# Way down of a SwiGLU network by seven products over all 22 tiles of h, with sums on GpSimd and raw stores

## The chip, the cores and the metric

The kernel runs on one core of one Trainium2 chip. The metric is device time in microseconds (us), the median of several runs; lower is better. The time before is 1420.02 us (three runs, 1419.3 to 1420.16).

A core has five engines, each with its own queue that it works off strictly in order: TensorE (PE in the profile: matrix products, with PEld for its weight loads), VectorE (DVE), ScalarE (ACT), GpSimd (POOL) and SyncE (SP), which here issues every DMA. Engines wait for each other by semaphores. TensorE writes its products into PSUM, which has eight banks of 128x512 floats; everything else on chip lies in SBUF, in tiles of 128 partitions by 1024 floats.

## The reference, cut to what matters

One layer of an encoder: two attention branches, a gated merge, an output projection, a LayerNorm, and then a SwiGLU network with a second LayerNorm. The change lies in the last three lines:

```python
x = layer_norm(DEEPNORM_ALPHA * x + mix, ln1_g[l], ln1_b[l])       # (1024, 1024)
gu = x @ w_ffn_in[l]                                               # the way up: (1024, 5632)
g, u = jnp.split(gu, 2, axis=-1)
ffn = (jax.nn.silu(g) * u) @ w_ffn_out[l]                          # the way down: h (1024, 2816) @ (2816, 1024)
x = layer_norm(DEEPNORM_ALPHA * x + ffn, ln2_g[l], ln2_b[l])
```

## The kernel before, in words

**Products.** Every product of floats is made of three products of rounded parts: an operand a is split into a high part (a cast on ACT) and a low part (a minus its high part, a subtraction), and hi*hi, hi*lo and lo*hi are added up in PSUM. `split` (L109 to L111) is that pair: `scalar.copy` on ACT, `tensor_tensor` subtract on DVE. Two blocks by two blocks are multiplied by seven block products in place of eight (the variant of Strassen's scheme by Winograd): the operands are first added and subtracted in a chain of four sums a side, and the seven products, numbered 1 to 7 here, are then added into the results. Part of the adding is left to PSUM: products 1, 6, 7 and 4 run on in one bank ("sx", "dx"), 5 and 3 in another ("sz", "dz"), and each intermediate value is read out of the bank between two of them.

**Way up** (`up_steps`, `pair_steps`, `run_pairs`). The 22 tiles of h (128 rows of h transposed, 1024 tokens wide; f = 0 to 21) are made one after the other. f = 0 is made by plain products, each other f by seven products of 12 matmuls each, in the order 1, 2, 6, 5, 7, 3, 4 (`pair_steps`, L183 to L231). Product 5 writes the bank "sz"; ACT copies it out (`p5`, COPY gt<-szf, L212); product 3 goes on in the same bank, so it waits for that copy. While f is multiplied, the weights of the next tiles are loaded by SP and made ready: the right-hand block wRf comes in by one DMA (L142), and its quarter wcf is cast on ACT (`prep_last`, CAST wcf<-wRf). After product 4 of f the last half of h is finished on ACT and DVE (L1306, L1307).

**Between the two.** h does not fit beside the rest, so it goes to DRAM. For the 16 tiles f = 2 to 17 (eight pairs, four groups of two in `SEVEN`) `left_sums` makes the left-hand sums of the pair (f, f + 1) with four subtractions or additions on DVE, splits each of the seven sums on ACT and DVE, and stores high and low parts side by side. The work of a pair is cut into 11 `pieces`; `next_piece` runs one of them after each product of the way up. f = 0, 1 and 18 to 21 are stored as they are (`h_dr`).

**Way down** (L1438 on). Tiles 0 and 1 are multiplied plainly (`down_plain`, eight tiles of 128 tokens, both halves of 512 columns), then the four groups of `SEVEN` by `down_seven`: a group is two pairs, taken twice (two token tiles of each half at a time), 7 products of 2 x 12 matmuls. The stored left sums are loaded ready for use (`load_left`), the right sums are made on chip a group ahead (`right_sums`, one sum of a pair on GpSimd, L1485, the others on DVE). DVE adds every bank into the sum of x and the result (`add_to`, L1460). Tiles 18 to 21 come last, plainly; with each of the eight token tiles done, its LayerNorm follows (`layer_norm`): statistics and one scaling on DVE, one scaling on ACT and one addition on GpSimd (L1195); the last tile ends on DVE alone.

**What sets the order.** The program is recorded line by line and a scheduler then orders the instructions of each engine by what it expects to be ready; a slot in SBUF or a bank in PSUM that is used again makes its new writer wait for the last reader. A GpSimd operation that overwrites a tile also waits until a DMA that stores that tile has read it.

Of the kernel before, what the change touches and what calls it, by code (L numbers as in the profile page):

```python
# [18 lines left out]
P = 128  # L19
# [29 lines left out]
def hybrid_trunk_kernel(ctx: ExitStack, tc, x, xt, w_first, w_v, w_in, b_gate, rel_bias, w_proj,  # L49
# [51 lines left out]
    h_dr = dram("h_dr", NF)  # L101


    SEVEN = [(f0, f0 + 2) for f0 in (2, 6, 10, 14)]
    ORDER = (1, 2, 6, 5, 7, 3, 4)
    s_dr = [[dram(f"s_dr{g}_{hf}_", 7) for hf in range(2)] for g in range(4)]
# [1070 lines left out]
    def layer_norm(t, g, b, name, quick, done=lambda cs: None, n_st=2, cuts=(LO, HI)):  # L1177
# [3 lines left out]
        for j in range(n_st):  # L1181
            nc.vector.bn_stats(st[:, 6 * j:6 * j + 6], t[:, j * w:(j + 1) * w])
            if j == 0:
                nc.vector.tensor_scalar(st[:, 2:3], st[:, 2:3], EPS * D, None, ALU.add)
# [96 lines left out]
    def plain_rest():  # L1281
        plain_half(HI, ops_21 + ops_1[4])
        dma(h_dr[0], first_h[1])

    def up_steps(f):
# [13 lines left out]
        def done(name, acc):  # L1299
            if name == "11":  # L1300
                nc.scalar.activation(c("11"), c("11"), AF.Silu)
            elif name == "12":
                nc.vector.tensor_tensor(c("12"), c("12"), c("11"), ALU.mult)
            elif name == "21":
                h = tl["h"]
                nc.scalar.activation(h[:, HI], acc, AF.Silu)  # L1306
                nc.vector.tensor_tensor(h[:, HI], h[:, HI], c("22"), ALU.mult)  # L1307
                if f in pair_of:
                    h_tiles[f] = h
                    if f % 2:  # L1310
                        pieces.extend(left_sums(f - 1))
                else:
                    dma(h_dr[f], h)
# [4 lines left out]
    pair_of = {f + d: (g, i) for g, fs in enumerate(SEVEN) for i, f in enumerate(fs)  # L1318
               for d in range(2)}
    h_tiles, pieces = {}, []  # L1320

    def left_sums(f):

        g, i = pair_of[f]
        a, b = h_tiles.pop(f), h_tiles.pop(f + 1)

        def out(p, src):
            def piece():
                o = slot("op", f"sl{f}_{p}", F32R)
                o4 = o.rearrange("p (t k c) -> p t k c", t=2, k=2)  # L1330
                split(o4[:, :, 0, :], o4[:, :, 1, :], src.rearrange("p (t c) -> p t c", t=2))
                for hf, cs in enumerate((LO, HI)):
                    dma(s_dr[g][hf][ORDER.index(p)][:, i * HW:(i + 1) * HW],
                        o[:, cs].bitcast(F32))
            return piece

        def put(dst, in0, in1, op):
            return lambda: nc.vector.tensor_tensor(dst, in0, in1, op)
# [7 lines left out]
    def next_piece(i):  # L1346
        if pieces:
            pieces.pop(0)()
# [91 lines left out]
    acc_t = [slot("op", f"x1_{tt}") for tt in range(8)]  # L1440

    def load_plain(f0, f1, tags):
        hs = []
        take = lambda name, dtype: cycle(tags, name, dtype)
        for f in range(f0, f1):
            hs.append(load_w(h_dr[f], f"h{f}", of("gt"), take, nc.vector) +
                      load_w(w_ffn_out[f * P:(f + 1) * P, :], f"fo{f}", of("gt"), take,
                             nc.vector))
        return hs

    def down_plain(hs, tt, evac, cuts=((0, HW), (HW, D))):
        ts_ = slice(tt * P, (tt + 1) * P)
        for n, (c0, c1) in enumerate(cuts):
            cs = slice(c0, c1)
            acc = bank(("mm", "tr", "sc")[n], f"fps{hs[0][0].name}_{tt}_{n}")[:, 0:c1 - c0]
            mm3(acc, [(hh[:, ts_], hl[:, ts_], oh[:, cs], ol[:, cs]) for hh, hl, oh, ol in hs])
            evac(acc_t[tt][:, cs], acc)

    def add_to(dst, acc):
        nc.vector.tensor_tensor(dst, acc, dst, ALU.add)  # L1460

    def right_sums(g, Ws, tags):

        def take(name):
            return cycle(tags, name, F32R)

        def split_to(W, key, src, nm):
            W[key] = take(f"{nm}h"), take(f"{nm}l")
            split(*W[key], src)

        def load(f, tag, cs):
            t = slot(tag, f"wd{tag}{f}")
            for j, dst in enumerate((LO, HI)):
                dma(t[:, dst], w_ffn_out[(f + j) * P:(f + j + 1) * P, cs])
            return t

        sub = ALU.subtract
        put = nc.vector.tensor_tensor
        for f, W in zip(SEVEN[g], Ws):

            L, R = load(f, "gt", LO), load(f, "yt", HI)
            split_to(W, "12", L, f"wdl{f}")
            yield
            put(L[:, LO], R[:, LO], L[:, LO], sub)
            nc.gpsimd.tensor_tensor(R[:, LO], R[:, HI], R[:, LO], sub)  # L1485
            yield
            c = W["c"] = take(f"wdc{f}")
            split(c[:, LO], c[:, HI], R[:, HI])
            yield
            put(R[:, HI], R[:, HI], L[:, LO], sub)  # L1490
            put(L[:, HI], L[:, HI], R[:, HI], sub)
            yield
            split_to(W, "54", L, f"wda{f}")
            yield
            split_to(W, "76", R, f"wdb{f}")
            yield

    def load_left(g, hf):
        ls = {}
        for n, p in enumerate(ORDER):  # L1500
            t = ls[p] = cycle(LEFT, f"sd{g}_{hf}_{p}", F32R)
            dma(t.bitcast(F32), s_dr[g][hf][n])
        return ls

    def down_seven(g, hf, Ws, ls, between):

        bx, by = {}, {}
        key = {1: ("12", LO), 2: ("12", HI), 5: ("54", LO), 4: ("54", HI), 7: ("76", LO),
               6: ("76", HI)}
        for p in ORDER:  # L1510
            for j in range(2):
                tt = 2 * hf + j
                nm = f"{g}_{tt}"
                up, lo = acc_t[tt], acc_t[tt + 4]
                if p == 1:
                    bx[j] = bank(("mm", "tr")[hf], f"dx{nm}")
                elif p in (2, 5):
                    by[j] = bank("sc" if p == 5 else ("tr", "pv")[j], f"d{'yz'[p == 5]}{nm}")
                acc = by[j] if p in (2, 5, 3) else bx[j]
                first = p in (1, 2, 5)  # L1520
                for i, W in enumerate(Ws):
                    if p == 3:
                        wh, wl = W["c"][:, LO], W["c"][:, HI]
                    else:
                        wh, wl = (w[:, key[p][1]] for w in W[key[p][0]])
                    o = i * HW + j * P
                    lh, ll = ls[p][:, o:o + P], ls[p][:, o + 256:o + 256 + P]
                    for n, (a, b) in enumerate(((lh, wh), (lh, wl), (ll, wh))):
                        mm(acc, a, b, start=(first and i == n == 0), stop=(i == n - 1 == 1),  # L1529
                           skip_group_check=not first)  # L1530
                for dst in {1: [up[:, LO]], 2: [up[:, LO]], 6: [up[:, HI]], 5: [lo[:, HI]],
                            7: [lo[:, HI]], 3: [up[:, HI]], 4: [lo[:, LO]]}[p]:
                    add_to(dst, acc)
            between()

    LEFT = ("bw",) * 4 + ("kp",) + ("bw",) * 5 + ("kp",) * 3
    right_tags = [QKV * 2 + ("pt",) * 4 + ("xt",) * 2, ("xt",) * 14]
    first = load_plain(0, 2, ("bw", "bw", "kp", "kp", "bw", "bw", "bw", "kp"))
    Wd = [[dict(), dict()] for _ in SEVEN]
    make = right_sums(0, Wd[0], right_tags[0])  # L1540
    for tt in range(8):
        dma(acc_t[tt], x1_dr[tt])
        down_plain(first, tt, lambda dst, acc: nc.vector.scalar_tensor_tensor(
            dst, dst, ALPHA, acc, ALU.mult, ALU.add))
        for _ in range(2):
            with tc.issue_after(added[0].ins):
                next(make, None)
    left = load_left(0, 0)
    for g in range(4):
        if g < 3:  # L1550
            make = right_sums(g + 1, Wd[g + 1], right_tags[(g + 1) % 2])
        for hf in range(2):
            ls = left
            if (g, hf) != (3, 1):
                left = load_left(g + hf, 1 - hf)
            down_seven(g, hf, Wd[g], ls, lambda: next(make, None))
    last = load_plain(18, NF, QKV * 2 + ("pt",) * 4 + ("bw",) * 4)
    norm2 = [bcast(src, slot("yt", f"ln2{n}")) for src, n in ((ln2_g, "g"), (ln2_b, "b"))]
    for tt in range(8):
        end = tt == 7  # L1560
# [46 lines left out]
```

## Time and profile before

| what | value |
|---|---|
| median of three runs | 1420.02 us (1419.3 to 1420.16) |
| span of the profiled execution | 1418.4 us |
| PE busy | 1408.0 us, 99% of the span |
| DVE busy | 1054.1 us, 74% |
| ACT busy | 684.7 us, 48% |
| POOL busy | 246.5 us, 17% |
| DMA | 276.54 MB, mean 195 GB/s |

The span runs from the first to the last instruction of the profiled execution; the page gives no other time of it. PE is busy in all but 10.4 us of the span, some 7 of them after its last matmul. The other engines' busy time costs nothing as long as PE never waits for it.

### The profile page before, as it was taken

What the parts mean: (1) busy time and instruction counts of PE and PEld (TensorE: products, weight loads), DVE (VectorE), ACT (ScalarE), POOL (GpSimd) and SP (SyncE); (2) the same over time, 40 slices, a digit from 0 to 9 for tenths busy, and PEclk for the clock granted to TensorE, in tenths of its full rate; (3) what the DMA queues carried; (4) which work ended last, traced back from release to release, by engine and by line L of the source; (5) the groups of instructions that cost most, each with busy time, mean ns of one, the idle gap of its engine ahead of it and who ended that gap; (6) DMA issues with size and microseconds to landing.
All of it is one profiled execution on the core that took longest, in us unless ns stands there. A gap on an engine that the chain in (4) does not pass through costs nothing.

```text
span 1418.4 us, 19023 instructions
## 1 busy us (share of the span) xinstructions
PE 1408.0 (99%) x6672; PEld 1171.7 (83%) x6672; DVE 1054.1 (74%) x1669; ACT 684.7 (48%) x1193; POOL 246.5 (17%) x318
## 2 busy tenths in 40 slices
PE   9999999999999999999999999999999999999997
PEld 7888888888888888888888888888888888888886
DVE  8967657535887778878998947777676656978757
ACT  6544444555888887874424624444344433212201
POOL 0000000002656888840001000000000000100014
PEclk9999999999999999999999999999999999999999
DMA  7486468846676469656651214444334458787502
GB/s 253 163 291 223 169 250 306 293 180 220 220 234 191 148 235 304 242 178 219 228 191 60 89 60 163 157 148 156 135 147 164 159 182 288 278 314 238 202 15 104
DMA packets 104974, 276.54 MB, mean 195 GB/s; under 512 B 10400, under 2 KB 26784, under 8 KB 104880
## 3 DMA queue, kind: packets, MB, share of 16 engines
q1 hardware_dynamic: 104880, 275.35, 55.4%
q8 instruction: 52, 0.85, 0.2%
q14 instruction: 42, 0.34, 0.1%
HBM read 179.33 MB, written 92.30 MB: 192 GB/s over the span
## 4 chain that ended last, share of the span: by engine, by line
PE 91%; DVE 2%; DMA 2%; ACT 1%; issue 1%; POOL 1%; SPq 0%; DVEq 0%; POOLq 0%; ACTq 0%
PE sxf L180 16%; PE sxp L180 9%; PE szf L180 8%; PE dx L1529 6%; PE v L482 5%; PE szp L180 4%; PE syf L180 4%; PE gps L607 4%; PE dz L1529 3%; PE ops L1375 3%; PE yAps L911 3%; PE syp L180 2%; PE tp_a L818 2%; PE tp_b L818 2%; PE fpswh_h L118 2%; PE fpswh_h L117 2%
## 5 line engine op out<-in xcount | busy, mean ns | idle before, releaser
L1485 POOL TENSOR_TENSOR wdyt<-wdyt 128x512 f32<-128x512 f32 x8 | 11.2, 1404 | 512.8 <-DMA sd<-s_dr 443.6
L795 POOL TENSOR_TENSOR w_b<-w_b,kp_b 128x511 f32<-128x511 f32 (+3 forms) x96 | 96.1, 1014 | 23.5 <-DVE kp_b L790 17.0
L790 DVE TENSOR_TENSOR_SCAN kp_b<-kp_b,ident_ps 128x512 f32<-128x512 f32 (+2 forms) x64 | 56.5, 885 | 21.2 <-ACT kp_b L787 20.3
L787 ACT ACTIVATE kp_b<-sc_b 128x512 f32<-128x512 f32 (+3 forms) x96 | 48.1, 501 | 28.0 <-PE sc_b L707 20.9
L180 PE MATMUL szf<-x1S63h,wcf 128*128 128x512 f32 x168 | 55.1, 389 | 0.0
L111 DVE TENSOR_TENSOR pt_b<-tp_b,pt_b 128x512 fp32r<-128x512 f32 (+1 forms) x96 | 49.9, 544 | 6.6 <-ACT pt_b L110 5.7
L730 POOL MEMSET bias<- 64x64 f32 x2 | 0.3, 144 | 313.7 <-ACT bias L726 313.7
L1460 DVE TENSOR_TENSOR x<-dx,x 128x512 f32<-128x512 f32 x64 | 43.4, 686 | 14.9 <-PE dx L1529 14.9
L111 DVE TENSOR_TENSOR sl<-h,sl 128x512 fp32r<-128x512 f32 x56 | 38.4, 686 | 20.5 <-ACT sl L110 20.5
L110 ACT CAST sl<-h 128x512 fp32r<-128x512 f32 x56 | 34.7, 619 | 36.9 <-PE syf L180 17.1
L760 POOL TENSOR_SCALAR w_a<-w_a,st_a 128x640 f32<-128x640 f32 (+2 forms) x64 | 42.2, 667 | 50.4 <-PE sc_a L707 27.0
L110 ACT CAST pt_b<-tp_b 128x512 fp32r<-128x512 f32 (+1 forms) x96 | 46.6, 502 | 8.2 <-PE tp_b L818 8.0
L1186 POOL TENSOR_TENSOR mv<-mv,neghalf 128x1 f32<-128x1 f32 x16 | 12.2, 760 | 220.6 <-DVE mv L1185 220.5
L1306 ACT ACTIVATE h<-sxf 128x512 f32<-128x512 f32 x21 | 12.6, 598 | 77.0 <-PE sxf L180 77.0
L755 ACT ACTIVATE w_a<-w_a,st_a 128x640 f32<-128x640 f32 (+2 forms) x64 | 44.7, 699 | 8.6 <-DVE st_a L749 7.5
L788 ACT ACTIVATE w_b<-sc_b 128x511 f32<-128x511 f32 (+3 forms) x96 | 48.2, 502 | 0.0
L818 PE MATMUL tp_b<-ident,w_b 128*128 128x128 f32 x288 | 47.3, 272 | 0.4 <-DVE pt_b L111 0.2
L111 DVE TENSOR_TENSOR pt_a<-tp_a,pt_a 128x512 fp32r<-128x512 f32 (+1 forms) x96 | 44.6, 485 | 3.3 <-ACT pt_a L110 2.2
L818 PEld LDWEIGHTS tp_b<-ident,w_b 128*128 128x128 f32 x288 | 36.4, 140 | 11.3 <-DVE pt_b L111 1.3
L110 ACT CAST pt_a<-tp_a 128x512 fp32r<-128x512 f32 (+1 forms) x96 | 39.3, 430 | 11.5 <-PE tp_a L818 10.6
L818 PE MATMUL tp_a<-ident,w_a 128*128 128x128 f32 x240 | 42.9, 275 | 0.4 <-DVE pt_a L111 0.3
L607 PE MATMUL gps<-xl,wh_g 128*128 128x512 f32 x96 | 41.7, 434 | 0.0
(1789 smaller groups left out, 4815.2 us busy)
## 6 DMA issues: line engine op xcount, KB each, us to landing
s_dr<-sl SPq DMA_DIRECT2D x112, 256.0 KB, 2.3
sd<-s_dr SPq DMA_DIRECT2D x56, 512.0 KB, 4.9
wLf<-in_w_ffn_in_dram SPq DMA_DIRECT2D x22, 512.0 KB, 4.3
wRf<-in_w_ffn_in_dram SPq DMA_DIRECT2D x22, 512.0 KB, 3.6
v_dr<-vc SPq DMA_DIRECT2D x16, 512.0 KB, 3.2
qs<-q_dr SPq DMA_DIRECT2D x16, 512.0 KB, 6.6
kh<-k_dr SPq DMA_DIRECT2D x16, 512.0 KB, 5.7
kl<-k_dr SPq DMA_DIRECT2D x16, 512.0 KB, 7.1
```

The lines of the kernel that those rows point to most:

```text
L110: return (nc.scalar.copy(dst_h, src), nc.vector.tensor_tensor(dst_l, src, dst_h.bitcast(F32), ALU.subtract))
L111: nc.vector.tensor_tensor(dst_l, src, dst_h.bitcast(F32), ALU.subtract))
L180: mm(acc, lw[:, ks], rx, start=(first and kt == i == 0), stop=(kt == 3 and i == 2), skip_group_check=not first)
L482: mm(accs[j], a, b, start=(first and kt == n == 0), stop=(kt == 3 and n == 2), skip_group_check=True)
L607: mm(acc[hf], lw[:, ks], rx[k][:, (LO, HI)[hf]], start=(k == j == 0), stop=(k == KT - 1 and j == 2))
L755: nc.scalar.activation(s[:, 0:w], s[:, 0:w], AF.Exp, bias=st[:, m:m + 1], scale=-1.0, accum_out=st[:, 2:3])
L787: nc.scalar.activation(kp[:, c0:e], sc[:, 0:n], AF.Sigmoid, scale=-1.0)
L788: nc.scalar.activation(be[:, m0:e], sc[:, m0 - c0:n], AF.Sigmoid)
L790: nc.vector.tensor_tensor_scan(kp[:, 0:e], kp[:, 0:e], ident_ps()[:, 0:e], 0.0, ALU.mult, ALU.add)
L795: nc.gpsimd.tensor_tensor(be[:, m0:e], be[:, m0:e], kp[:, m0 - 1:e - 1], ALU.mult)
L818: ins = tr(tp[:, (qb - lo_q) * P:(qb - lo_q + 1) * P], wt[qb - q0][:, (kb - qb) * P:(kb - qb + 1) * P], ident)
L1529: mm(acc, a, b, start=(first and i == n == 0), stop=(i == n - 1 == 1), skip_group_check=not first)
```

## The change

- All 22 tiles of h now go through seven products: 11 pairs in `GROUPS` of 3, 4 and 4 pairs. A group runs its seven products in the order 1, 2, 5, 3, 6, 7, 4, each over all pairs of the group and four tiles of tokens (`steps`, 21 of them). `down_plain`, `down_seven`, `load_plain` and `h_dr` are gone.
- The left sums of all 11 pairs are made on GpSimd, and they are stored raw, not split: a half as large store for each of the seven. `next_piece` runs two pieces at a time.
- On the way down each raw sum is loaded two steps ahead (`load_left`), cast on ACT and its low part subtracted on GpSimd (`left_piece`). The right sums are made and split one step ahead (`right_piece`).
- All four banks of a kind are held through a group. Group 0's first read of each sum scales x by alpha (`take_down`).
- The LayerNorms of token tiles 0 to 3 follow product 6 of the last group, those of tiles 4 to 7 product 4, the last product; the last one is taken in two halves of 256 columns in the same bank.
- `w_ffn_out` is laid out on the host so that one load brings a pair's two blocks.

```diff
+    GROUPS = ((0, 3), (3, 7), (7, 11))
+    ORDER = (1, 2, 5, 3, 6, 7, 4)
...
         def out(p, src):
-            def piece():
-                o = slot("op", f"sl{f}_{p}", F32R)
-                o4 = o.rearrange("p (t k c) -> p t k c", t=2, k=2)
-                split(o4[:, :, 0, :], o4[:, :, 1, :], src.rearrange("p (t c) -> p t c", t=2))
-                for hf, cs in enumerate((LO, HI)):
-                    dma(s_dr[g][hf][ORDER.index(p)][:, i * HW:(i + 1) * HW],
-                        o[:, cs].bitcast(F32))
-            return piece
+            return lambda: dma(s_dr[g][p][:, i * HW:(i + 1) * HW], src)
         def put(dst, in0, in1, op):
-            return lambda: nc.vector.tensor_tensor(dst, in0, in1, op)
+            return lambda: nc.gpsimd.tensor_tensor(dst, in0, in1, op)
         a_lo, a_hi, b_lo, b_hi = a[:, LO], a[:, HI], b[:, LO], b[:, HI]
         return [out(1, a_lo), out(4, b_hi),
                 put(b_hi, a_hi, b_hi, ALU.add), put(a_hi, a_lo, a_hi, ALU.subtract),
...
     def next_piece(i):
-        if pieces:
-            pieces.pop(0)()
+        for _ in range(2):
+            if pieces:
+                pieces.pop(0)()
...
+    def left_piece(s, i):
+        g, p = steps[s]
+        src = left_raw[s][i]
+        o = slot("xt", f"sl{g}_{p}_{i}", F32R)
+        nc.scalar.copy(o[:, LO], src)
+        nc.gpsimd.tensor_tensor(o[:, HI], src, o[:, LO].bitcast(F32), ALU.subtract)
+        lefts.setdefault(s, []).append(o)
+
+    def right_piece(s, i):
+        g, p = steps[s]
+        sub, put = ALU.subtract, nc.vector.tensor_tensor
+        L, R = raw[g, 0][i], raw[g, 1][i] if p not in (1, 2) else None
+        if p == 5:
             put(L[:, LO], R[:, LO], L[:, LO], sub)
+        elif p == 3:
             nc.gpsimd.tensor_tensor(R[:, LO], R[:, HI], R[:, LO], sub)
+        elif p == 6:
             put(R[:, HI], R[:, HI], L[:, LO], sub)
+        elif p == 4:
             put(L[:, HI], L[:, HI], R[:, HI], sub)
+        t, cs = {1: (L, LO), 2: (L, HI), 5: (L, LO), 3: (R, HI), 6: (R, HI), 7: (R, LO),
+                 4: (L, HI)}[p]
+        o = cycle(RIGHT, f"wd{g}_{p}_{i}", F32R)
+        split(o[:, LO], o[:, HI], t[:, cs])
...
+    for s, (g, p) in enumerate(steps):
+        n = GROUPS[g][1] - GROUPS[g][0]
...
+        if s + 2 < len(steps):
+            load_left(s + 2)
...
+        todo = prepare(s + 1) if s + 1 < len(steps) else []
...
+        for j in range(4):
...
+            for cs in (slice(0, 256), slice(256, HW)) if end else (LO,):
+                for i in range(n):
+                    lh, ll = (lefts[s][i][:, c:c + HW][:, ts_] for c in (0, HW))
+                    wh, wl = (rights[s][i][:, c:c + HW][:, cs] for c in (0, HW))
+                    for k, (a, b) in enumerate(((lh, wh), (lh, wl), (ll, wh))):
+                        mm(accs[j][:, cs], a, b, start=(first and i == k == 0),
+                           stop=(i == n - 1 and k == 2), skip_group_check=not first)
+                take_down(g, p, j, accs[j], cs)
+            for _ in range(-(-len(todo) // (4 - j))):
+                todo.pop(0)()
+            if s < 3:
+                next_piece(0)
+            if last and p in (6, 4):
+                tt = j + 4 * (p == 4)
+                layer_norm(acc_t[tt], *norm2, f"2_{tt}", end,
...
```

What the scheduler makes of this, at three places.

SP's queue on the way up, from the load of wRf15 on. In these names wRf and wLf are weight blocks, s_dr a stored left sum, sl12_5 a split sum before (pair 12 and 13, product 5), h12 and h13 the tiles that the sums are made in now. Before:

```order
L142 DMA wRf15_10072<-in_w_ffn_in_dram 128x1024
L131 DMA wLf16_10111<-in_w_ffn_in_dram 128x1024
L1333 DMA s_dr2_0_2_187<-sl10_6_9973 128x512
L1333 DMA s_dr2_1_2_194<-sl10_6_9973 128x512
L1333 DMA s_dr2_0_5_190<-sl10_3_9992 128x512
L1333 DMA s_dr2_1_5_197<-sl10_3_9992 128x512
L1333 DMA s_dr2_0_0_185<-sl12_1_10052 128x512
L1333 DMA s_dr2_1_0_192<-sl12_1_10052 128x512
L1333 DMA s_dr2_0_6_191<-sl12_4_10091 128x512
L1333 DMA s_dr2_1_6_198<-sl12_4_10091 128x512
L142 DMA wRf16_10219<-in_w_ffn_in_dram 128x1024
```

and now:

```order
L141 DMA wRf15_9881<-in_w_ffn_in_dram 128x1024
L130 DMA wLf16_9917<-in_w_ffn_in_dram 128x1024
L1325 DMA s_dr1_2_143<-h13_9807 128x512
L1325 DMA s_dr1_4_148<-h13_9807 128x512
L1325 DMA s_dr1_5_144<-h13_9807 128x512
L1325 DMA s_dr1_7_147<-h12_9678 128x512
L1325 DMA s_dr1_6_146<-h12_9678 128x512
L1325 DMA s_dr1_3_145<-h13_9807 128x512
L141 DMA wRf16_10014<-in_w_ffn_in_dram 128x1024
```

The load of wRf16 stood behind the first two sums of the pair (12, 13); it now stands behind all of that pair's sums, the last of which needs all four of GpSimd's operations.

ACT's queue at the same place, in f = 14 (gt14<-szf14 is the copy of product 5 that product 3 waits for, wcf16 the cast of a quarter of wRf16). Before:

```order
L208 COPY h14_10130<-sxf14_10057 128x512
L110 CAST sl12_2_10180<-h13_9990 128x2x256
L212 COPY gt14_10070<-szf14_10133 128x512
L110 CAST sl12_7_10199<-h12_9843 128x2x256
L110 CAST wcf16_10235<-wRf16_10219 128x512
```

and now:

```order
L109 CAST waf15h_9893<-taf15_9883 128x1024
L207 COPY h14_9937<-sxf14_9866 128x512
L109 CAST wcf16_10030<-wRf16_10014 128x512
L211 COPY gt14_9879<-szf14_9941 128x512
L109 CAST wlf17h_10050<-wLf17_10048 128x1024
```

The cast of wcf16 has moved ahead of the copy of gt14. The same pair of rows stands so in f = 4, 6, 8, 10, 12, 14, 16 and 18, eight times; in the odd ones the copy comes first.

DVE's queue in the first group of the way down (x1_2 is token tile 2 of the sum, d2_0_2 the bank of product 2 in group 0 for that tile, wd0_6_0 the low part of the right operand of product 6, pair 0). Before, in the first group of `down_seven`:

```order
L1460 TENSOR_TENSOR x1_0_11134<-dy0_0_11406,x1_0_11134 128x512
L1460 TENSOR_TENSOR x1_1_11135<-dy0_1_11414,x1_1_11135 128x512
L111 TENSOR_TENSOR wda6l_11474<-wdgt6_11396,wda6h_11473 128x1024
L1460 TENSOR_TENSOR x1_0_11134<-dx0_0_11380,x1_0_11134 128x512
L111 TENSOR_TENSOR wdb6l_11492<-wdyt6_11399,wdb6h_11491 128x1024
```

and now:

```order
L1499 TENSOR_TENSOR x1_1_10872<-d2_0_1_11022,x1_1_10872 128x512
L110 TENSOR_TENSOR wd0_6_0_11161<-wd1_0_10897,wd0_6_0_11161 128x512
L110 TENSOR_TENSOR wd0_6_1_11178<-wd1_1_10898,wd0_6_1_11178 128x512
L110 TENSOR_TENSOR wd0_6_2_11195<-wd1_2_10899,wd0_6_2_11195 128x512
L1499 TENSOR_TENSOR x1_2_10873<-d2_0_2_11040,x1_2_10873 128x512
L110 TENSOR_TENSOR wd0_7_0_11225<-wd1_0_10897,wd0_7_0_11225 128x512
L1499 TENSOR_TENSOR x1_3_10874<-d2_0_3_11055,x1_3_10874 128x512
L110 TENSOR_TENSOR wd0_7_1_11241<-wd1_1_10898,wd0_7_1_11241 128x512
L110 TENSOR_TENSOR wd0_7_2_11257<-wd1_2_10899,wd0_7_2_11257 128x512
L110 TENSOR_TENSOR wd1_1_3_11408<-wd0_6_11145,wd1_1_3_11408 128x512
L1496 SCALAR_TENSOR_TENSOR x1_4_10875<-x1_4_10875,d5_0_0_11073 128x512
```

Seven subtractions from SBUF now stand ahead of the first read of product 5 (d5_0_0), whose bank product 3 goes on in.

More of the change, by code (lines that the diff above doesn't have):

```diff
@@ L1459, in add_to @@
[L1459 to L1483, printed above, removed]
+    raw_tags = ((("gt",) * 3, ("kp",) * 3), (("yt",) * 3 + ("bw",), ("gt",) * 3 + ("pt",)),
+                (("kp",) * 4, ("yt",) * 3 + ("bw",)))
@@ L1495, in right_sums @@
[L1495 to L1534, printed above, removed]
```

149 lines of the change are left out of this document (79 added, 70 removed).

## The prediction

> **What bounds the kernel now.** I read the page first, then the busy time by stretches, then the chain that ended last, then single instructions around the places that the change touches.
>
> ```profile
> span 1418.4 us, 19023 instructions
> ...
> PE 1408.0 (99%) x6672; PEld 1171.7 (83%) x6672; DVE 1054.1 (74%) x1669; ACT 684.7 (48%) x1193; POOL 246.5 (17%) x318
> ...
> POOL 0000000002656888840001000000000000100014
> ```
>
> PE is busy in all but 10.4 us of the span. GpSimd does nothing from slice 24 to 33: that is the whole way up, where the change now gives it work. The stretches (way up, the two plain tiles, the seven-product groups, the last tiles):
>
> ```profile
> core 0: us, PE busy (x) PEld busy (x) DVE busy (x) ACT busy (x) POOL busy (x), PEclk, DMA share, GB/s
> 821.50:1160.00 338.50, 338.50 (x1495) 279.99 (x1494) 231.32 (x317) 140.22 (x212) 0.00 (x0) 1.00 0.41 148
> ...
> 1214.00:1367.00 153.00, 153.00 (x677) 126.58 (x676) 119.38 (x164) 28.51 (x30) 8.41 (x6) 1.00 0.66 234
> 1367.00:1418.00 51.00, 44.04 (x206) 36.80 (x204) 37.23 (x62) 8.07 (x7) 21.18 (x15) 0.98 0.21 83
> ```
>
> PE has no gap on the way up nor in the groups, at the full clock (1.00). So a product less is a gain, and any new wait of PE is a loss, each at its full length. The chain that ended last, around f = 16:
>
> ```profile
> 1038.16 5.44 PE sxf L180 x24
> 1043.60 2.72 PE syf L180 x12
> ...
> 1054.48 2.72 PE szf L180 x12
> ```
>
> Twelve matmuls take 2.72 us, 0.2267 each. The first row is product 4 of f = 15 and product 1 of f = 16, which starts at 1040.88; product 3 of f = 16 starts at 1054.48, 13.60 us later.
>
> **Products saved.** Before, the way down has 96 matmuls for tiles 0 and 1, 672 in the groups and 192 for tiles 18 to 21, counted as 512 columns each: 960. Now 7 products x 11 pairs x 4 token tiles x 3 are 924. The 36 saved are 36 x 0.2267 = **-8.2 us**. DVE also loses the splits of the left sums on the way up, worth nothing, since PE does not wait there.
>
> **The shared way into SBUF.** The new work is on GpSimd, beside DVE. What the two do to each other stands in the timeline of before:
>
> ```profile
> 1217.38 1.62 POOL L1485 TENSOR_TENSOR wdyt<-wdyt 128x512 f32<-128x512 f32 x1 [10.68 <-DVE wdgt L1484]
> 1217.77 0.68 DVE L1460 TENSOR_TENSOR x<-dx,x 128x512 f32<-128x512 f32 x1
> ...
> 1258.46 0.68 DVE L111 TENSOR_TENSOR wdc<-wdyt,wdc 128x512 fp32r<-128x512 f32 x1
> 1258.68 1.63 POOL L1485 TENSOR_TENSOR wdyt<-wdyt 128x512 f32<-128x512 f32 x1 [14.65 <-DVE wdgt L1484]
> ...
> 1293.25 0.68 DVE L1460 TENSOR_TENSOR x<-dx,x 128x512 f32<-128x512 f32 x1
> 1293.46 1.29 POOL L1485 TENSOR_TENSOR wdyt<-wdyt 128x512 f32<-128x512 f32 x1 [11.36 <-DVE wdgt L1484]
> 1293.85 1.46 DVE L111 TENSOR_TENSOR wdc<-wdyt,wdc 128x512 fp32r<-128x512 f32 x1
> 1295.23 0.68 DVE L1460 TENSOR_TENSOR x<-dx,x 128x512 f32<-128x512 f32 x1
> 1295.83 0.68 DVE L1490 TENSOR_TENSOR wdyt<-wdyt,wdgt 128x512 f32<-128x512 f32 x1
> ```
>
> A read of a bank (x<-dx,x) keeps its 0.68 us beside GpSimd. A subtraction with both operands in SBUF does not: begun 0.39 us into GpSimd's 1.29, it takes 1.46, the rest of GpSimd's operation and then its own time. The other way round GpSimd, begun 0.22 into DVE's, takes 1.63, its own 1.29 and what was left of DVE's. So each holds the other off for a whole operation: 1.29 us on GpSimd, 0.60 on DVE (the last two rows start 0.60 apart). I call this the port.
>
> [...] The rows show it at 512 columns alone; if 1024-wide subtractions held GpSimd only as long as these, 0.60, the wait of the next paragraph would be 2.4 us in place of 3.4.
>
> **Way up: a wait in every second tile.** The order shows wRf of the next even tile behind all stores of a pair's sums on SP, and its cast ahead of the copy on ACT that product 3 waits for. The links, from the rows of f = 15 and 16:
>
> ```profile
> 1040.92 0.60 ACT L1306 ACTIVATE h<-sxf 128x512 f32<-128x512 f32 x1 [5.41 <-PE sxf L180]
> 1041.55 0.69 DVE L1307 TENSOR_TENSOR h<-h,gt 128x512 f32<-128x512 f32 x1 [1.93 <-ACT h L1306]
> 1049.01 1.22 DVE L111 TENSOR_TENSOR wbf15l<-tbf,wbf15h 128x1024 fp32r<-128x1024 f32 x1
> 1050.75 1.22 DVE L111 TENSOR_TENSOR waf15l<-taf,waf15h 128x1024 fp32r<-128x1024 f32 x1
> 1051.80 0.59 ACT L212 COPY gt<-szf 128x512 f32<-128x512 f32 x1 [0.36 <-PE szf L180]
> 1056.04 0.62 ACT L110 CAST wcf<-wRf 128x512 fp32r<-128x512 f32 x1 [1.74 <-DVE sl L111]
> ```
>
> ```profile
> s_dr<-sl SPq DMA_DIRECT2D x112, 256.0 KB, 2.3
> ...
> wRf<-in_w_ffn_in_dram SPq DMA_DIRECT2D x22, 512.0 KB, 3.6
> ```
>
> Counted from the start of the even tile's product 1 (1040.88): the odd tile's h is done at 1.4 (1041.55 + 0.69). Its upper half is stored; GpSimd's first sum overwrites that half and waits for the store, 2.3 us (to 3.7). Four sums of 1.29 with 0.1 of handing over each are 5.6 (9.3); that hand-over is my estimate (L1306's end and L1307's start are 0.03 apart, product 5's end and the copy L212 0.04, and a semaphore to SP and back is longer). DVE's two 1024-wide subtractions (1.22) fall among them, at 8.1 and 9.9 in these rows, and hold them up by 1.1 each (11.5). The last store is issued, about 0.4, then the load (11.9), which lands 3.6 later (15.5). The cast takes 0.62, the copy 0.59, with some 0.3 of handing over: 17.0. Product 3 was due at 13.6. So PE waits **3.4 us**, eight times (f = 4, 6, ..., 18): **+27 us**. Behind the waiting cast on ACT stands only that copy; behind the stores on SP stand wRf and the next wLf, which has time. In before the same copy ran at 1051.80, ahead of the cast at 1056.04: nothing waited. From below: no wait at the port (-2.2) and the shortest chain otherwise (-0.5) leave 0.7 each, 5.6 in all; from above: a load as slow as 4.6, with two more wide subtractions' ends in the way, 4.5 each, 36.
>
> **Start of the way down: port-bound.** After f = 21's product 1 frees the first slots (2.72 us from that tile's start), load and cast bring GpSimd's first subtraction at about 6. By the order, up to DVE's first read of product 5, which product 3 needs, GpSimd has 23 operations (4 of them the sums of the last pair) and DVE some 26 subtractions with both operands in SBUF: 23 x 1.29 + 26 x 0.60 = 45.3 us of port. So that read ends at 6 + 45.3 + 0.7 = 52. PE would be there at 19.04 (f = 21) + 3 products x 36 x 0.2267 (8.16) = 43.5. **+9 us** (0 if the port's queue is packed around PE's needs, 14 if every hand-over costs 0.1 more).
>
> **Rest of the way down.** For a group of four pairs, port time is GpSimd 28 + 4 operations x 1.29 = 41.3 and DVE 28 + 12 x 0.60 = 24.0, 65.3 us beside 76.2 of PE. So the debt of group 0 is not passed on much; while it is worked off I put **+5** (0 to 15: at the upper end one step in two of the 14 waits for 2 us).
>
> **The tail.** The last tiles of before end so:
>
> ```profile
> 1409.89 2.37 POOL L1195 TENSOR_TENSOR x<-x,ln2b 128x1024 f32<-128x1024 f32 x1 [2.04 <-ACT x L1194]
> ...
> 1410.77 0.28 PE L120 MATMUL fpswh_h<-wh_fo,wl_h 128*128 128x256 f32 x1
> ...
> 1412.07 0.26 DVE L1185 BATCH_NORM_AGGREGATE mv<-bn 128x2 f32<-128x24 f32 x1
> ...
> 1412.41 0.55 POOL L1186 TENSOR_TENSOR mv<-mv,neghalf 128x1 f32<-128x1 f32 x1
> ...
> 1413.78 1.41 DVE L1190 SCALAR_TENSOR_TENSOR x<-x,mv,ln2b 128x512 f32<-128x512 f32 x2
> ```
>
> ```profile
> L1182 DVE BATCH_NORM_STATS2 bn<-x 128x6 f32<-128x512 f32 x14 | 9.7, 695 | 0.5
> L1187 DVE SCALAR_TENSOR_TENSOR x<-x,mv,ln2g 128x1024 f32<-128x1024 f32 x8 | 10.5, 1307 | 0.3
> ```
>
> Before, 7.4 us pass from the last matmul's end (1410.77 + 0.28) to the end of the span, 3.2 of them behind DVE's last scaling, and a token tile has 5.44 us of PE to cover its LayerNorm. Now tiles 4 to 7 get 2.72 each in the last product, while DVE stays behind: by its order, between the end of tile 4's matmuls and the read of tile 7's first half stand 3 reads (0.60), 5 statistics (0.7), 5 small ones (0.26) and 2 scalings (1.31), 9.2 us. So that read begins at 2.72 + 0.3 + 9.2 = 12.2 after the product's start. Tile 7's second half uses the same bank and waits for it (0.4), then takes 12 x 0.113: PE ends at 14.0 in place of 4 x 2.72 = 10.9, +3.1. Then the port: the two last GpSimd additions (2.37) and DVE's scaling of tile 7 between them exclude each other, and GpSimd's power for tile 7 stands behind both: 14.0 + 2.37 + 1.31 + 2.37 + 0.55 = 20.6, then 1.41 on DVE and 3.2 for the last store, 25.2. Before's pattern would give 10.9 + 7.4 = 18.3. **+7** (2 to 9).
>
> **Sum.** -8.2 + 27 + 9 + 5 + 7 = +39.8, on the profiled 1418.4: 1458.2. The median of the runs lies 1.6 above that span, so 1459.8; I give 1460.
>
> **Rivals.** *The port costs little*: GpSimd and DVE run side by side. Then the way up has 5.6, the start of the way down nothing, the tail its wait for the bank: -8.2 + 5.6 + 3.1 = +0.5, 1420.5. For it speaks that the reads of banks are not slowed; against it stand the rows with 1.46 and 1.63.
>
> *Faster*: as that, and wRf lands in time. The place is product 3 of the even tiles, the price 8 x 0.7, and it decides at 13.6 us: a chain of 14.3 without the port needs only 0.7 less, such as sums that follow each other without hand-over (0.4) and a store of 2.0. Then -8.2 + 3.1 gives 1415. It needs the port to be free, so it is unlikely.
>
> *Half*: the subtractions of DVE fall beside the sums and not among them. The way up costs 8 x 1.2, group 0 half, the rest 2: -8.2 + 9.6 + 4.5 + 2 + 6 = +14, 1434.
>
> *Port-bound to the end*: over the whole way down the port has 92 x 1.29 + 110 x 0.60 = 185 us, and the last LayerNorms add 7 x (2.37 + 1.2) = 25: 210 beside 924 x 0.2267 = 209 of PE. If hand-overs cost 0.1 in each of these 200, the way down is 20 longer: 1480.
>
> **How the numbers follow.** Forecast (1445 to 1472) 0.63, half 0.15, to the end 0.13, little port 0.05, faster 0.04. The range takes the forecast's bounds and the nearer part of both neighbours: 1437 to 1475. Below about 0.2% (2.8 us) a difference from no change can't be told here. Faster 0.04, within 0.2% 0.03 (most of the little-port case), slower 0.93.
>
> **What would show it.** Right: in the profile after, PE has gaps of about 3.4 us before product 3 of f = 4, 6, ..., 18, ended by ACT's copy, whose engine waited for wRf's DMA; DVE subtractions of 512 columns on the way down take up to 1.9; PE waits at product 3 of group 0 for DVE; the last matmul lies some 10 us before the end. Wrong: no gap on the way up (the load came in time), or DVE subtractions of 0.68 beside GpSimd's operations, or a way down whose length is 209 us and no more.

## The result, and the profile after

The changed kernel takes 1470.01 us (median of four runs, 1465.44 to 1471.84) beside 1420.09 us for the kernel before: a ratio of 1.0345, 95% interval 1.0326 to 1.0364. It is 50 us slower; the profiled execution has a span of 1470.1 us, 51.7 more than before.

From the page of the changed kernel, the busy times and GpSimd's busy tenths:

```profile
PE 1424.1 (97%) x6636; PEld 1179.0 (80%) x6636; DVE 1023.9 (70%) x1563; ACT 698.6 (48%) x1247; POOL 450.5 (31%) x442
...
POOL 0000000004557797700010111110011114866656
```

PE has 36 matmuls less and is busy 16 us longer. That is the first odd thing; a wait alone does not make PE busier. To see where, I cut both kernels at the same matmuls: way up from f = 1, way down, and what follows the last matmul. The columns are those of the prediction's stretches; behind the five engines' busy times stand the granted clock, the DMA share and GB/s. Before:

```profile
792.74:1193.06 400.32, 400.22 (x1765) 330.77 (x1764) 271.07 (x367) 166.72 (x246) 0.00 (x0) 1.00 0.43 154
1193.06:1411.05 217.99, 217.98 (x973) 180.73 (x971) 173.71 (x247) 44.33 (x46) 30.64 (x22) 1.00 0.56 201
1411.05:1418.40 7.35, 0.00 (x0) 0.00 (x0) 3.83 (x6) 0.00 (x0) 1.76 (x2) 0.81 0.37 143
```

and after:

```profile
792.62:1239.61 446.99, 420.42 (x1765) 343.00 (x1764) 227.82 (x284) 141.90 (x202) 81.54 (x49) 0.95 0.32 110
1239.61:1459.76 220.15, 213.57 (x937) 175.41 (x935) 186.24 (x223) 82.01 (x144) 148.85 (x96) 0.98 0.43 141
1459.76:1470.10 10.34, 0.00 (x0) 0.00 (x0) 4.37 (x8) 1.06 (x1) 5.82 (x3) 0.73 0.39 152
```

The way up is 46.7 us longer, the way down 2.2, the end 3.0. Of the 46.7, 26.6 are waits (446.99 - 420.42), and 20.2 are the same 1765 matmuls taking longer, at a mean granted clock of 0.95 in place of 1.00. The waits by name, on PE from 790 us on (total, times, longest):

```profile
PE szf L179 <- ACT gt L211: 24.2, 8, 3.3
PE d L1537 <- DVE x L1496: 4.0, 1, 4.0
PE d L1537 <- DVE x L1499: 2.5, 3, 2.1
PE sxf L179 <- DVE gt L194: 2.3, 1, 2.3
```

Eight waits before product 3, as forecast. The chain that ended last, in f = 4:

```profile
850.32 0.61 ACT h L1307
...
850.95 0.70 DVE h L1308
...
851.66 2.00 DMA s_dr<-h
...
853.91 1.42 POOL h L1328
...
855.40 1.30 POOL h L1328
...
856.78 2.17 POOL h L1328
...
859.02 2.16 POOL h L1328
861.20 0.32 SPq L1325
...
861.62 4.08 DMA wRf<-in_w_ffn_in_dram
...
865.73 0.62 ACT wcf L109
866.35 0.49 ACT gt L211
...
866.88 4.60 PE szf L179 x12
```

Read it from the top: h is done, its half is stored, GpSimd makes four sums (two of them 2.2 us where another takes 1.30: they start 0.35 and 0.86 us into 1024-wide subtractions on DVE, 856.43 to 857.78 and 858.16 to 860.03, and end 1.2 behind each), SP issues the last store and then the load, ACT casts and at last copies. Every link is the forecast's. The last row is not: product 3 takes 4.60 us instead of 2.72. The stretch of 3.41 us in which PE waits, the next and the one after it, and below them another wait of the same kernel (2.6 us before product 3 of f = 6) that falls half into one stretch and half into the next:

```profile
863.71:867.12 3.41, 0.40 (x2) 0.24 (x2) 0.74 (x2) 1.22 (x3) 0.00 (x0) 1.00 0.69 257
867.12:870.53 3.41, 3.41 (x9) 2.64 (x9) 0.55 (x1) 0.93 (x1) 0.00 (x0) 0.50 0.02 5
870.53:873.95 3.42, 3.42 (x16) 2.81 (x16) 2.42 (x3) 0.00 (x0) 0.00 (x0) 1.00 0.00 0
904.67:908.08 3.41, 2.19 (x10) 1.49 (x8) 0.00 (x0) 0.00 (x0) 0.00 (x0) 1.00 0.88 282
908.08:911.50 3.42, 2.04 (x9) 1.68 (x10) 1.29 (x2) 2.15 (x3) 0.00 (x0) 1.00 0.25 102
```

After a stretch with PE busy for 0.40 us the granted clock is 0.50 for exactly one stretch: 9 matmuls instead of some 15. After stretches with 2.19 and 2.04 it stays at 1.00.

### The profile page after: what moved, and what is told of

Same layout as the page of the kernel before. It is cut to its first block, busy times and chain, and to the rows that moved or that the text cites. A ratio compares the mean times of both kernels' runs of the same rounds, so it can differ in the third digit from the quotient of the medians.

```text
span 1470.1 us, 18953 instructions
## 1 busy us (share of the span) xinstructions
PE 1424.1 (97%) x6636; PEld 1179.0 (80%) x6636; DVE 1023.9 (70%) x1563; ACT 698.6 (48%) x1247; POOL 450.5 (31%) x442
## 4 chain that ended last, share of the span: by engine, by line
PE 80%; DMA 6%; DVE 5%; POOL 5%; ACT 2%; issue 1%; POOLq 0%; SPq 0%; DVEq 0%; ACTq 0%
PE d L1537 11%; PE sxf L179 10%; PE sxp L179 8%; PE szf L179 7%; PE v L481 5%; POOL h L1328 4%; PE gps L606 4%; PE szp L179 4%; PE yAps L910 3%; PE ops L1366 3%; DMA wRf<-in_w_ffn_in_dram 2%; PE syf L179 2%; PE syp L179 2%; PE tp_b L817 2%; PE tp_a L817 2%; DVE wd L110 2%
## 5 line engine op out<-in xcount | busy, mean ns | idle before, releaser
L1537 PE MATMUL d<-wd,sl 128*128 128x512 f32 (+1 forms) x936 | 213.6, 390 | 6.6 <-DVE x L1496 4.0
L1537 PEld LDWEIGHTS d<-wd,sl 128*128 128x128 f32 x936 | 175.6, 190 | 44.6 <-ACT wd L109 4.4
L1328 POOL TENSOR_TENSOR h<-h,h 128x512 f32<-128x512 f32 x33 | 59.8, 1813 | 372.8 <-DMA s_dr<-h 309.3
L1463 POOL TENSOR_TENSOR sl<-sr,sl 128x512 fp32r<-128x512 f32 x77 | 120.7, 1598 | 62.6 <-ACT sl L1462 62.6
L110 DVE TENSOR_TENSOR wd<-wd,wd 128x512 fp32r<-128x512 f32 x77 | 88.7, 1174 | 12.7 <-ACT wd L109 12.6
L179 PE MATMUL szf<-x1S63h,wcf 128*128 128x512 f32 x168 | 66.6, 462 | 24.2 <-ACT gt L211 24.2
L109 ACT CAST wd<-wd 128x512 fp32r<-128x512 f32 x77 | 45.9, 618 | 72.2 <-PE d L1537 53.9
L1462 ACT CAST sl<-sr 128x512 fp32r<-128x512 f32 x77 | 46.1, 618 | 50.0 <-POOL sl L1463 23.2
L179 PEld LDWEIGHTS szf<-x1S63h,wcf 128*128 128x128 f32 x168 | 37.9, 225 | 36.3 <-ACT gt L211 27.6
L1499 DVE TENSOR_TENSOR x<-d,x 128x512 f32<-128x512 f32 (+1 forms) x69 | 45.7, 673 | 20.9 <-PE d L1537 20.8
L194 DVE TENSOR_TENSOR h<-szf,h 128x512 f32<-128x512 f32 x21 | 14.5, 690 | 52.4 <-PE szf L179 36.7
```

Source lines behind the costliest of these rows:

```text
L109: return (nc.scalar.copy(dst_h, src), nc.vector.tensor_tensor(dst_l, src, dst_h.bitcast(F32), ALU.subtract))
L110: nc.vector.tensor_tensor(dst_l, src, dst_h.bitcast(F32), ALU.subtract))
L179: mm(acc, lw[:, ks], rx, start=(first and kt == i == 0), stop=(kt == 3 and i == 2), skip_group_check=not first)
L1328: return lambda: nc.gpsimd.tensor_tensor(dst, in0, in1, op)
L1463: nc.gpsimd.tensor_tensor(o[:, HI], src, o[:, LO].bitcast(F32), ALU.subtract)
L1537: mm(accs[j][:, cs], a, b, start=(first and i == k == 0), stop=(i == n - 1 and k == 2), skip_group_check=not first)
```

## The experiments

The theory: the queue order (copy behind cast, cast behind load, load behind the sums' stores) makes the waits on the way up; GpSimd's operations next to DVE's make those at the start of the way down; and the clock, halved after a wait, is a loss of its own. The rivals: GpSimd itself slows what PE needs, the stores hold the load, DVE becomes the bound, or product 3 is slow for a reason of its own. All edits are made to the changed kernel.

**The copy first.** Only two rows of ACT's queue change places, eight times.

```diff
-            nc.scalar.copy(c("22"), st["sz"])
+            copied[:] = [nc.scalar.copy(c("22"), st["sz"])]
...
-        if f > 1:
+        if f > 3:
+            with tc.issue_after(copied[0].ins):
+                prep_last(Wf[f], f"f{f}", "op")
+        elif f > 1:
             prep_last(Wf[f], f"f{f}", "op")
```

> The only edit: the cast of the quarter wcf stands behind the copy of product 5 on ACT; GpSimd's sums, the stores and the load of wRf keep their places. Theory (the copy waits only because it stands behind a cast that waits for a load behind the stores): the waits of about 3.1 us before product 3 go. DVE's low part of wcf still stands ahead of the addition that product 4 waits for, so a wait of about 1.6 comes there in the same eight tiles, too short for the clock to be halved. Gain 8 x 1.5 of waiting and 17 of half clock: about 1441 us. Rival (GpSimd's sums slow down what product 3 needs, whatever the order): the waits stay, 1465 to 1475.

Measured 1439.84 us (ratio to before 1.0138, 1.0123 to 1.0153). The chain around f = 12 then:

```profile
1020.88 4.20 DMA wRf<-in_w_ffn_in_dram
...
1025.11 0.63 ACT wcf L109
...
1025.76 0.61 DVE wcf L110
1026.37 0.69 DVE gt L194
...
1027.11 5.76 PE sxf L179 x24
```

The same load lands as late as before, and now DVE is caught behind it: its low part of wcf stands ahead of the addition that product 4 waits for. PE's waits for it (total, times, longest; one of the nine is that of f = 21):

```profile
PE sxf L179 <- DVE gt L194: 10.4, 9, 2.1
```

No stretch of the way up has a halved clock. 30 us came back from a swap of two rows, though the waits of the way up shrank by only 16, from 26.5 to 10.4; PE's busy time there fell by 17.5 as well, from 420.42 to 402.93 us. The way down lost 2.1 us again (222.26 for 220.15): the wait before product 3 of group 0 is 5.8 us in this run and not 4.0.

**Copy and sum first.** The same for DVE:

```diff
             add(c("22"), st["sx"])
+            added7[:] = added
...
+            with tc.issue_after(copied[0].ins), tc.issue_after(added7[0].ins):
```

> As the run with the copy first, and DVE's low part of wcf also stands behind the addition that product 4 waits for. GpSimd still makes the sums, and the load of wRf still stands behind their stores. Theory (the sums on GpSimd are harmless as long as nothing that PE needs soon stands behind that load): the 10.4 us that PE waited for that addition go, and the way up is as long as before: 1429 us, within 2 of the run with the sums on DVE. Rival (GpSimd holds DVE off at the shared way into SBUF, so that PE gets its reads late anyway): waits of 0.5 to 1 in most tiles stay, 1434 to 1440.

Measured 1428.12 us (1.0055, 1.0042 to 1.0069). PE's waits from 790 us on:

```profile
PE d L1541 <- DVE x L1503: 3.4, 3, 2.1
PE d L1541 <- ACT wd L109: 2.8, 1, 2.8
PE sxf L179 <- DVE gt L194: 2.0, 1, 2.0
```

No wait is left on the way up but that of f = 21. The sums are on GpSimd still, at the same place, and cost nothing ahead of f = 21, where PE waits for 2.0 us (0.6 in the run with the sums on DVE). The rival, that GpSimd holds up what PE reads, is out for the eight waits of the way up.

**Sums on DVE.**

```diff
-            return lambda: nc.gpsimd.tensor_tensor(dst, in0, in1, op)
+            return lambda: nc.vector.tensor_tensor(dst, in0, in1, op)
```

> The only edit: the left sums of the way up are made on DVE again, with the raw stores. Theory (four GpSimd operations of 1.3 to 2.2 us push the load of wRf past the point where product 3 is due): four sums of 0.6 us on DVE bring the load forward by 4 us, no wait on the way up, no halved clock there: 1470 - 25 - 17 = about 1428. The way down keeps its waits. Rival (the stores in SP's queue hold the load back, whatever engine makes the sums): the waits stay, 1460 or more.

Measured 1427.84 us (1.0056, 1.0041 to 1.0071), the same as the run before this one, and no wait is left before product 3: the chain can be cured at its other end too. But the edit changed more than the engine. In f = 14 SP now issues (x2 stands for two stores)

```profile
1002.58 1.94 SPq L1325 DMA_DIRECT2D s_dr<-h  x2
1006.05 0.33 SPq L141 DMA_DIRECT2D wRf<-in_w_ffn_in_dram  x1
```

so the scheduler has put the load behind two of the pair's stores and not behind all six; the other four follow it. Shorter sums and a better place of the load are not told apart here, and that the raw stores would be harmless ahead of the load is not shown. The cast still stands ahead of the copy, but is over in time. That the two runs agree to 0.3 us is partly chance: the way up is 2.8 us shorter here (401.09 for 403.85), the way down 2.6 longer (222.74 for 220.15).

**The wait filled.** Ten matmuls that nobody reads stand ahead of product 3 in f = 4, 6, ..., 18:

```diff
         def p3():
+            if nm in FILLED:
+                spare = bank("tr", f"fill{nm}")
+                for n in range(10):
+                    ins = mm(spare, W["hb"][0][:, 0:P], ops[4][0][0], start=True, stop=True)
+                    if n == 0:
+                        tc.keep_in_program_order(ins)
             product(st["sz"], W, ops, 3, False)
```

> Ten matmuls whose result is not used are added ahead of product 3 in f = 4, 6, ..., 18, into a bank of their own: 80 more matmuls, 2.27 us a tile, in the time in which PE waits. Theory (the halved clock after the wait comes from PE having been idle for more than about half of a 3.4 us stretch): the wait shrinks from 3.1 to about 0.8, product 3 keeps 2.72 us instead of 4 to 4.6, and the kernel gets faster by 14 to 18 us although it does more work: 1452 to 1456. Rival (product 3 is slow there for another reason, such as its freshly cast operand or the traffic at that time): product 3 stays at 4 us and more, 1468 to 1475.

Measured 1455.97 us (1.0252, 1.0236 to 1.0267): 14 us faster with 80 matmuls more. The chain and the load are as they were (ACT's copy in f = 4 ends at 866.36 us, 866.84 before); only product 3 is not:

```profile
866.40 3.06 PE szf L179 x12
```

3.06 us in place of 4.60, and no stretch of the way up is halved. So it is PE's own idling, 1.4 us at most before product 3 in this run and up to 3.3 in the changed kernel, that halves the clock, not the fresh operand and not the traffic.

**The wait filled by degrees.** As the run before this one, but with 1 matmul in f = 4, 2 in f = 6, up to 8 in f = 18.

```diff
+    FILLED = {f"f{f}": f // 2 - 1 for f in range(4, 19, 2)}
```

> The kernel after, with 1, 2, ..., 8 unused matmuls ahead of product 3 in f = 4, 6, ..., 18, so that PE idles about 2.9, 2.7, 2.5, 2.2, 2.0, 1.8, 1.6 and 1.3 us there. Theory (the clock is halved for a 3.41 us stretch of a fixed grid when PE was busy in less than about 0.42 of the stretch before it): halving is possible only where more than 1.98 us of the pause fall into one stretch, so at most in f = 4 to 12 and not in all of these, never in f = 14, 16 and 18; two to four halvings, about 1460 us. Rival (the length of the pause alone decides): the halvings are exactly the longest pauses, however they lie on the grid.

Measured 1455.41 us in a single run, so without an interval. There was one halved stretch on the way up, in f = 12, and not two to four at 1.7 us each; the time came out 5 us below what I expected, in part for that reason. But the halving is not at the longest pause. f = 4 (its two stretches first) paused for 2.83 us from start to start of a matmul, f = 12 for 2.71:

```profile
861.49:864.90 3.41, 1.58 (x7) 0.97 (x6) 0.00 (x0) 0.54 (x2) 0.00 (x0) 1.00 1.00 323
864.90:868.32 3.42, 2.80 (x12) 2.35 (x13) 1.29 (x2) 1.62 (x3) 0.00 (x0) 1.00 0.04 12
1028.74:1032.15 3.41, 1.21 (x5) 1.04 (x6) 1.29 (x2) 2.16 (x3) 0.00 (x0) 1.00 0.38 154
1032.15:1035.57 3.42, 3.42 (x9) 2.65 (x9) 0.11 (x1) 0.00 (x0) 0.00 (x0) 0.50 0.00 0
```

PE busy for 1.58 of 3.41 us keeps the clock, 1.21 halves it. In the changed kernel itself the wait of 2.3 us in f = 21 halved the clock (from 1235.76 us on), and that of 2.6 in f = 6 did not. What counts is how much of the pause falls into one stretch; the rival is out.

**Left low parts on DVE**, on the way down:

```diff
-        nc.gpsimd.tensor_tensor(o[:, HI], src, o[:, LO].bitcast(F32), ALU.subtract)
+        nc.vector.tensor_tensor(o[:, HI], src, o[:, LO].bitcast(F32), ALU.subtract)
```

> The only edit: the low parts of the left sums on the way down are subtracted on DVE instead of GpSimd. Theory (the two engines hold each other off, so that an operation that takes 1.3 us on GpSimd and 0.6 on DVE should be on DVE): group 0 no longer waits; 6 us of waiting and 4 of half clock go there: about 1459. Rival (DVE becomes the bound of the way down, its reads queue behind 77 more subtractions): 1472 to 1480.

Measured 1458.28 us (1.0267, 1.025 to 1.0284). The two groups of subtractions, first with GpSimd (mean ns behind the busy time), then with DVE alone:

```profile
L1463 POOL TENSOR_TENSOR sl<-sr,sl 128x512 fp32r<-128x512 f32 x77 | 120.7, 1598 | 62.6 <-ACT sl L1462 62.6
L110 DVE TENSOR_TENSOR wd<-wd,wd 128x512 fp32r<-128x512 f32 x77 | 88.7, 1174 | 12.7 <-ACT wd L109 12.6
```

```profile
L110 DVE TENSOR_TENSOR wd<-wd,wd 128x512 fp32r<-128x512 f32 x77 | 54.4, 719 | 6.0 <-ACT wd L109 5.9
L1463 DVE TENSOR_TENSOR sl<-sr,sl 128x512 fp32r<-128x512 f32 x77 | 53.5, 703 | 8.3 <-ACT sl L1462 8.2
```

With 77 operations more, DVE needs 107.9 us for what took it 88.7, and GpSimd's 120.7 are gone. DVE is not the bound. PE's wait of 4.0 us for DVE's first read of product 5 has shrunk to 0.4; one of 1.1 for ACT's cast is new.

Not all of the 11.7 us is the edit's. Of the 10.9 between the two profiled spans, 4.5 lie on the way down (215.61 for 220.15) and 5.5 on the way up, which the edit leaves as it was:

```profile
792.29:1233.73 441.44, 416.02 (x1765) 339.92 (x1764) 227.23 (x288) 141.99 (x202) 73.13 (x43) 0.97 0.32 111
```

The waits there are 25.4 us (26.6 in the changed kernel), but nine stretches were halved and not twelve, so PE is busy 4.4 us less. That the expected 1459 was met is luck to that extent.

**Both on DVE**, the two edits together.

> Left sums of the way up and left low parts of the way down both on DVE; the seven products over all 22 tiles stay. Theory (two separate losses that add): 1427.8 less the 11.7 that the low parts gave alone, 1416 us, 0.3% below the kernel before. Rival (with all of it, DVE is the bound at the start of the way down, which also has the last pair's sums): 1420 to 1427.

Measured 1418.12 us (0.9988, 0.9979 to 0.9997), where 1416 was expected: on top of the sums on DVE the low parts bring 9.7 us, alone 11.7. That the two figures are so near is partly chance, since they come from different places: here the way down alone is 10.6 us shorter (212.16, 222.74 with only the sums on DVE), there it was 4.5. So that the gains add is not shown. From 790 us on, PE waits 0.2 us in f = 21 and 2.1 at the end, and never is the clock halved before the last matmul. What is left of the gain is small, since the end keeps most of it.

**The last tile whole**, with both on DVE:

```diff
-            for cs in (slice(0, 256), slice(256, HW)) if end else (LO,):
+            for cs in (LO,):
```

> As the run with both on DVE, and the last token tile is multiplied in one piece of 512 columns and not in two halves in one bank. Theory (at the end DVE's and GpSimd's LayerNorm steps are late, not PE): PE's wait of 2.1 us ahead of the second half goes and its last matmul ends some 2 to 3 us earlier, but the span ends within 1 us of that run. Rival (the wait for the bank is on the path that sets the end, as the prediction's tail counted it): 2 to 3 us faster.

Measured 1418.72 us (0.9992, 0.9983 to 1.0001). The way down and the end with two halves, then with one whole tile:

```profile
1192.41:1404.57 212.16, 210.01 (x937) 174.04 (x935) 184.06 (x299) 82.68 (x144) 33.59 (x21) 1.00 0.43 147
1404.57:1414.90 10.33, 0.00 (x0) 0.00 (x0) 4.37 (x8) 1.08 (x1) 5.83 (x3) 0.70 0.39 152
```

```profile
1194.13:1403.74 209.61, 209.60 (x925) 173.24 (x923) 181.72 (x293) 81.45 (x142) 31.56 (x19) 1.00 0.44 146
1403.74:1416.90 13.16, 0.00 (x0) 0.00 (x0) 7.22 (x14) 2.30 (x2) 7.93 (x5) 0.62 0.41 159
```

PE's way down is 2.55 us shorter, and what follows its last matmul takes 2.83 longer: 222.5 and 222.8 us together. PE's wait for the bank is not on the path that sets the end.

**The norms on DVE**, on top of that: `quick` (both scalings on DVE) for all eight tiles, the upper half's statistics first for tiles 4 to 7.

```diff
-                layer_norm(acc_t[tt], *norm2, f"2_{tt}", end,
+                layer_norm(acc_t[tt], *norm2, f"2_{tt}", True,
...
-                           4 if end else 2, late_low=end)
+                           4 if end else 2, late_low=p == 4)
```

> As the run with the last tile whole, and the last LayerNorms of all eight token tiles end on DVE (both scalings), so that neither ACT nor GpSimd has a 1024-wide step there; the statistics of the upper half of tiles 4 to 6 are taken first. Theory (at the end DVE's scalings and GpSimd's additions hold each other off, 2.4 us a tile): the time from PE's last matmul to the end falls from 13.1 to about 10.5, 1416 us, and 0.3% below the kernel before. Rival (DVE alone is the bound there, and gets 1.3 us more for each tile): 1419 to 1424.

Measured 1416.94 us (0.998, 0.9971 to 0.9989), the fastest of all and 0.2% below the kernel before. What follows the last matmul takes

```profile
1403.05:1414.80 11.75, 0.00 (x0) 0.00 (x0) 8.18 (x13) 0.00 (x0) 2.58 (x2) 0.63 0.36 134
```

11.75 us in place of 13.16, where I expected 10.5. So the edit takes 1.4 us off the end; it moves the scalings and additions and changes the order of the statistics at once, and their shares stay open. The rest of the late end, against 7.35 before, I put down to DVE's own work, which gets 2.72 us of PE a tile to hide under and no longer 5.44; no run tests that.

## Why the prediction was right, and where it was not

The forecast was 1460 in a range of 1437 to 1475; 1470.01 was measured. The sign, the place and the mechanism of the largest term were right, but the sum is right for a mixed reason: one term of 24 us was missing, and the others were together 12 too large. That they offset it was luck: with the missing term alone, 1484 would have come out, beyond the range. The signs named in advance are there (waits of 3.0 us on average, DVE's subtractions up to 1.85, the wait at product 3 of group 0, the last matmul 10.3 us before the end).

- **Products saved**, -8.2. Right: PE needs 209.60 us for the way down (the run with the last tile whole) where it needed 217.98, 8.4 less.
- **Way up, eight waits of 3.4**, +27. Right in place, number and cause (the runs with the order changed show the cause), 24.2 in size. Two terms of the 3.4 were the author's estimates, which no row of before shows: the 1.1 us by which a 1024-wide subtraction holds up a sum, and 0.1 for each hand-over. In f = 4 the two sums beside such subtractions took 2.17 and 2.16 us and another 1.30, some 0.9 more each; one sum followed another within 0.07 or 0.08 us, the first began 0.25 behind the store's landing.
- **"Any new wait of PE is a loss, each at its full length."** This step failed. A wait also halved the clock behind it: 20.2 us on the way up (420.42 busy for 400.22) and 3.6 on the way down (213.57 for the 210.01 of the run with both on DVE). On the way up a wait cost 1.8 times its length. The forecast read the clock's 1.00 off stretches in which PE never waits, and took it for a constant; its own row of 1367 to 1418 us, with PE idle for 7 us at the end, has 0.98.
- **Start of the way down**, +9. It was 2.3 in f = 21 and 4.0 before product 3 of group 0: 6.3. The port is the cause as far as the run with the low parts on DVE tells: DVE's subtractions fall from 1174 to 719 ns and the 4.0 goes to 0.4.
- **Rest of the way down**, +5. It was 0.4. With 65 us of port time beside 76 of PE in a group, the debt is simply worked off; I priced a wait that nothing in that sum called for.
- **Tail**, +7. It was 5.1: 2.1 before the second half and 3.0 behind the last matmul. The working was wrong in one link: it hung GpSimd's addition for tile 5 on PE's end. In the trace that addition follows ACT's scaling and starts at 1459.27 us, 0.5 ahead of PE's end, and the run with the last tile whole shows that PE's end does not matter. That a 1024-wide scaling and such an addition hold each other off was an estimate too, from rows of 512 columns; the trace has it: a scaling begun at 1431.93 us, 0.28 into an addition of 2.40, took 3.20 and not the 1.31 of the one at 1429.01, and an addition begun at 1436.80, 0.07 into a scaling, took 3.48.

Together: -8.4 + 0.4 for the last tile's two halves + 24.2 + 20.2 + 3.6 + 6.3 + 0.4 + 5.1 = +51.8, where the spans differ by 51.7.

Of the rivals, "the port costs little" and "half" had too little on the way up. "Port-bound to the end" gave 1480 and is as near to 1470.01 as the forecast, but not by its mechanism: the way down is 2.2 us longer than before, not 26 (its own price of 20 on top of the forecast's -8.2 + 9 + 5).

## What to carry to other kernels

When work moves to another engine, look at what is queued behind its stores: here a load stood behind them, a cast behind the load, and a copy that PE needed behind the cast; swapping two rows of one queue gave 30 us back. In the changed kernel the halved clock added 20.2 us, over twelve stretches of 3.41, to the 26.6 that PE waited on the way up: price a wait of the size seen here, 2 us or more, at its length and at up to 1.7 us for each halved stretch behind it. On the way down a subtraction that takes 1.3 us alone on an idle engine and holds off the busy one was dearer than 0.7 on the busy one, by 4.5 us of the way down for 77 of them.

## What the runs showed of the hardware

**The clock.** In the records of all these runs the granted clock changes only at points of a fixed grid of 3.41 us, and is 1.00 or 0.50. I worked out PE's busy share, by the profile's busy times, for every stretch of the eleven traces in which PE was busy for less than nine tenths and which, with the stretch after it, lies between 800 us and the last matmul; work at half clock counts half. All 34 stretches up to 0.417 were followed by a halved one, and none of the 55 from 0.428 up (14 and 5 of them in the changed kernel's own trace). The first two rows are the highest of the 34 and the stretch after it. In the third, a stretch at half clock, PE is busy for 2.80 us; that counts as 1.40 of 3.42 (0.41), and another halved one follows:

```profile
949.04:952.45 3.41, 1.42 (x6) 1.18 (x7) 1.29 (x2) 2.15 (x3) 0.00 (x0) 1.00 0.38 155
952.45:955.87 3.42, 3.42 (x10) 2.65 (x9) 0.46 (x1) 0.00 (x0) 0.00 (x0) 0.50 0.00 0
993.41:996.83 3.42, 2.80 (x7) 2.22 (x8) 1.29 (x2) 1.61 (x3) 0.00 (x0) 0.50 0.02 6
```

Counted so, four halved stretches with pauses of 0.6 to 1.0 us in them (PE busy for 2.80, 2.60, 2.43 and 2.80) come to 0.36 to 0.41, and each was followed by another: two stretches of 6.83 us together in f = 10, 12, 14 and 16. With a pause of 0.5 us in it (1170.91 to 1174.32, busy for 2.92, counted 0.428) it was not. A wait of 2.0 us was enough where all of it lay in one stretch (f = 21 of the run with the copy and the sum first, halved from 1194.13 us on), and the 2.6 us in f = 6 of the changed kernel cost nothing more, since the grid cut them in two.

No wait of the changed kernel on the way up was longer than 3.3 us, and seven of the eight before product 3 halved the clock.

The changed kernel's times scatter more than those of any other here, 1465.44 to 1471.84, and go with the mean granted clock (0.986 in the fastest run, 0.982 in the slowest). That the grid lies differently against the program in each run would do this; it was not tried.

**A small operation on GpSimd was held off by 1.0 us.** In the end of the changed kernel the power of one element a partition (it turns the variance into the scale) takes 0.55 us alone (at 1445.38 us), and 1.54 when it starts 0.45 us into DVE's 1024-wide scaling; another that starts 0.04 us into such a scaling (at 1451.53) still takes 0.55:

```profile
1456.01 1.58 DVE L1188 SCALAR_TENSOR_TENSOR x<-x,mv,ln2g 128x1024 f32<-128x1024 f32 x1
1456.46 1.54 POOL L1187 TENSOR_TENSOR mv<-mv,neghalf 128x1 f32<-128x1 f32 x1
```
